# Output weights in a room of their own: loaded, gated and split during the attention, with the first output products ahead of the second row of merge work

## The chip, the cores and the metric

One core of one Trainium2 chip. The metric is the device time of one launch in microseconds (us). Five engines work side by side, each through its own list of instructions in order: TensorE (PE, matrix products), VectorE (DVE), ScalarE (ACT), GpSimd (POOL) and SyncE (SP). SP computes nothing here: its list holds most of the transfers between the chip's main memory and the core's buffer, and a transfer that has to wait for a buffer holds up every transfer behind it in that list.

## The reference

One layer of a diffusion block over 2048 tokens of width 1024, with 256 context tokens. Cut to what matters:

```python
fx, qx, kx, vx = split_projection(hx @ w_in)
y_four = fourier_mix(fx)                                        # 2048 x 512
y_attn = neighbourhood_attention(qx, kx, vx, kc, vc, rpb)       # 2048 x 512, 8 heads
g_f, g_a = split(sigmoid(hx @ w_gate))
merged = g_f * (y_four @ w_fourier_out) + g_a * (y_attn @ w_attn_out)
x = x + g1 * (merged @ w_out)                                   # w_out: 1024 x 1024
hx2 = modulate(rms_norm(x, norm2_g), sh2, sc2)
x = x + g2 * (relu(hx2 @ w_mlp1) ** 2 @ w_mlp2)
```

A factor of a product is kept as two f16 tiles, a high part H and a low rest L, and a product is made of three matmuls (H by H, H by L, L by H).

## The kernel before

The program runs in stages: projections, Fourier mixer, attention, merge, MLP. Loops in Python write the whole program out, a scheduler with a timeline of its own then sets the order on each engine; at run time each engine goes through its list in order and waits on semaphores. What is said below of orders is what the built program holds.

**Attention.** 64 steps (head pair 0 to 3, block of rows 0 to 3, block of columns 0 to 3), each with two heads. A head's block runs: scores `sc` on PE, bias and minimum on DVE (line 1312, tile `s`), exponential on ACT (1316), transposes `tp` on PE, high part `pH` on ACT, low part `pL` on DVE (1333), values `pv` on PE, scaling `yp` on ACT (1342). The queries of a block of rows are eight transfers, `Q` and `Ql` of two heads, put into SP's list one step of four ahead by `fetch`, which chains its transfers in program order.

**Filler.** Between the blocks a generator, `beside_attention`, yields small pieces of other work: first the Fourier half of the merge (`pmf`), then `load_wa`, then `attn_out(0)`. `load_wa` brings the four blocks of `w_attn_out` through the staging tile `wst`, of which there are two buffers, and scales and splits them on POOL:

```python
def load_wa():
    for k in range(4):
        wt = pm.tile([128, D], F32, tag="wst", name=f"wao{k}", bufs=2)
        fetch(wt, a["w_attn_out"][0, k * 128:(k + 1) * 128, :])
        pool.tensor_scalar(wt, wt, mgs[:, 0:1], None, op0=ALU.mult)
        pool.tensor_copy(wa[0][:, k, :], wt)
        pool.tensor_tensor(wa[1][:, k, :], wt, wa[0][:, k, :], op=ALU.subtract)
```

**Merge.** The 2048 tokens are cut into eight rows of W = 256. `attn_out(t)` loads the attention's result of row t into a `wst` buffer (`yat`), splits it (`yaH`, `yaL`), makes eight products `pua` (12 matmuls of 128x256 each), and forms the gated sum as `mH`, `mL`, with `gf`, `ft` and `ga` loaded for each pair of products. `out_proj(t, i)` multiplies half a row with the output weights: two products `po` of 24 matmuls of 128x512, added to `x1` (a tile of x) on DVE, stored, and normed on ACT. `norm_T(t)` transposes the normed row and writes the MLP's input. In steady state the loop runs out_proj(t), attn_out(t+2), norm_T(t).

**The output weights.** `wo` holds `w_out` times the gate `g1r` as H and L, in the pool `pg`, which is opened only when the attention's pools are closed. Eight blocks `wou0` to `wou7` of 512 KB are staged in `wst` and in `xh`, multiplied on DVE (line 1534), copied to H on ACT (1535), and subtracted to L on POOL or DVE in turn (1536). This stands in program order between the pieces of `attn_out(1)`; `out_proj(0, 0)` comes after it.

**Start of the MLP.** Four of seven parts of its input (`hc`) have room early. The other three, and the two `raw` buffers for weights still to be prepared, lie in the pool `pr`, opened when `pg` is closed.

Of the kernel before, what the change touches and what calls it, by code (L numbers as in the profile page):

```python
# [19 lines left out]
D = 1024  # L20
# [43 lines left out]
def dit_block(ctx: ExitStack, tc: tile.TileContext, a, out, taps=None, upto=9):  # L64
# [3 lines left out]
    def sbuf(name, side="left"):  # L68
        return tc.alloc_tile_pool(name=name, bufs=1, side=side, reuse_waits="tile")
# [7 lines left out]
    def mm3(ps, ops, start=True, stop=True):  # L77
        n = 3 * len(ops)
        i = 0
        for lh, ll, rh, rl in ops:  # L80
            for l, r in ((lh, rh), (lh, rl), (ll, rh)):
                last_mm[0] = pe.matmul(ps, l, r, start=(start and i == 0), stop=(stop and i == n - 1))  # L82
                i += 1
# [964 lines left out]
    def fetch(dst, src):  # L1048

        with tc.issue_after(in_order[0].ins):  # L1050
            in_order[0] = sp.dma_start(dst, src)
# [301 lines left out]
            act.dma_start(yA[hp, :, rb * 512:(rb + 1) * 512], yo)  # L1353

    W = 256
    pm = wa = None
    merged = {}

    def attn_out(t, ps_pool, m_pool):
# [35 lines left out]
            pool.tensor_tensor(wa[1][:, k, :], wt, wa[0][:, k, :], op=ALU.subtract)  # L1395
# [62 lines left out]
    def out_proj(t, i):  # L1458
        mH, mL = merged[t]
        r0 = t * W + i * 128  # L1460
        nm = f"{t}_{i}"
        cs = slice(i * 128, (i + 1) * 128)
        x1 = x1s.pop(0)
        load_x1()
        for n in range(2):
            ns = slice(n * 512, (n + 1) * 512)
            ps = mmp.tile([128, 512], F32, tag="mm", name=f"po{nm}_{n}")
            mm3(ps, [(mH[:, k, cs], mL[:, k, cs], wo[0][:, k, ns], wo[1][:, k, ns]) for k in range(KT)])
# [50 lines left out]
        put(1, b21)  # L1519

    NT = S // W
    def stage_wo(k):

        p_, tag = ((pm, "wst"), (pg, "xh"))[k % 2]
        t = p_.tile([128, D], F32, tag=tag, name=f"wou{k}", bufs=2)
        sp.dma_start(t, a["w_out"][0, k * 128:(k + 1) * 128, :])
        return t


    attn = attn_out(1, mmp, pg)  # L1530
    for k in range(8):
        next(attn)
        wt = stage_wo(k)
        dve.tensor_tensor(out=wt, in0=wt, in1=g1r, op=ALU.mult)
        act.activation(wo[0][:, k, :], wt, AF.Copy)
        (pool, dve)[k % 2].tensor_tensor(out=wo[1][:, k, :], in0=wt, in1=wo[0][:, k, :], op=ALU.subtract)  # L1536
    for _ in attn:
        pass
    load_x1()
    load_x1()  # L1540
    for t in range(NT - 2):
        out_proj(t, 0)
        out_proj(t, 1)
        for _ in attn_out(t + 2, mmp, pg):
            pass
        norm_T(t)
    pm.release()

# [8 lines left out]

    def load_hc(half, part, then=None):
        r = {}
        for c in (PRODUCTS[:4], PRODUCTS[4:])[part]:  # L1560
# [135 lines left out]
    def small(name):  # L1696
        return pr.tile([128, 512], F32, tag="wo", name=name, bufs=5)

    prep = prepare(jobs, lambda n_: pr.tile([128, 2048], F32, tag="raw", name=n_, bufs=2), lambda n_: pr.tile([128, 512], F32, tag="wt", name=n_),
                   lambda n_: small(n_).bitcast(F16).rearrange("p (c n) -> p c n", c=1), 1, act.dma_start, pool.dma_start)  # L1700
    acc, banks = {}, {}

# [84 lines left out]
    for i, s in enumerate(slots):  # L1787
# [20 lines left out]
    for p_ in (pr, p2p, pl, mmp):  # L1808
        p_.release()


# [52 lines left out]
```

## Time and profile before

| what | us |
|---|---|
| runs | 2658.70, 2662.83, 2666.41 (median 2662.83) |
| the profiled execution, its own time | 2660.88 |
| its span, first to last instruction | 2659.1 |
| PE busy in the span | 2538.6 (95%) |
| DVE, ACT, POOL busy | 1827.3, 1183.3, 484.4 |
| last low part `pL` of the attention begins | 1213.28 |
| first matmul of `attn_out(2)`, start of the steady merge | 1261.34 |
| first matmul of the MLP | 1482.09 |

The profiled execution lies 1.95 us under the median, and 1.8 us of its time lie outside its span. All places in time below are from the span's start. PE's row counts matmuls as they overlap, so that 95% does not say that PE runs at its best; idle time of PE is what the waits and the windows are read for.

### The profile page before, as it was taken

The numbers are of one execution on the slowest core, as the hardware profiler recorded it, in microseconds if no ns is written. First come the engines' busy times: TensorE is split into PE (matmuls) and PEld (weight loads), VectorE is DVE, ScalarE is ACT, GpSimd is POOL, SyncE is SP. The second block draws the span as 40 slices with busy tenths as digits, with TensorE's granted clock in tenths as the row PEclk, the third lists the DMA queues.
The fourth block names the chain that finished last, engine by engine and source line by source line (L and its number), as shares of the span: only waits on it lengthen the run. The fifth ranks groups of instructions, "written<-read, shape, count | busy, mean of one in ns | idle before, by whom it ended". The sixth has DMA issues, their size and how long they took to land.

```text
span 2659.1 us, 42665 instructions
## 1 busy us (share of the span) xinstructions
PE 2538.6 (95%) x15830; PEld 1473.0 (55%) x15830; DVE 1827.3 (69%) x3672; ACT 1183.3 (44%) x2113; POOL 484.4 (18%) x715
## 2 busy tenths in 40 slices
PE   6899989898999899998999999999999999999999
PEld 5445756776656678875666444444444444444444
DVE  6756976568553678887777696978877644636367
ACT  5623225545242577874444564627351333314050
POOL 1201221012224545452000121121211100000000
PEclk9999999999999999998999999999999999999999
DMA  8577689867374744556767777787766533333334
GB/s 269 137 225 204 203 248 304 270 204 245 93 249 141 199 118 138 148 169 207 237 226 264 260 242 261 231 279 233 268 235 230 181 99 105 101 103 99 104 103 155
DMA packets 345962, 517.77 MB, mean 195 GB/s; under 512 B 48497, under 2 KB 210505, under 8 KB 341401
## 3 DMA queue, kind: packets, MB, share of 16 engines
q1 hardware_dynamic: 296425, 406.50, 48.8%
q0 software_dynamic: 29104, 75.23, 8.4%
q10 hardware_dynamic: 20224, 33.31, 3.9%
q8 instruction: 124, 2.03, 0.3%
q14 instruction: 85, 0.70, 0.1%
HBM read 370.11 MB, written 145.84 MB: 194 GB/s over the span
## 4 chain that ended last, share of the span: by engine, by line
PE 68%; DMA 11%; DVE 11%; issue 3%; ACT 3%; POOL 3%; SPq 2%; DVEq 0%; ACTq 0%; POOLq 0%
PE p L82 21%; PE pm L82 17%; PE ps_g L82 8%; PE po L82 6%; DMA w12m<-in_w_mlp 3%; PE pua L82 2%; PE ps_k L82 2%; PE tp L1325 2%; PE pmf L1263 2%; PE pv L1339 1%; SPq L188 1%; PE ps_f L82 1%; PE ps_v L82 1%; PE sc L1303 1%; DVE wo L387 1%
## 5 line engine op out<-in xcount | busy, mean ns | idle before, releaser
L82 PE MATMUL pm<-hc,wb 128*128 128x512 f16 x2688 | 582.6, 379 | 5.6 <-DVE p L1605 2.1
L82 PE MATMUL p<-wb,a 128*128 128x512 f16 x2688 | 581.9, 379 | 2.1 <-DVE X L1605 1.5
L82 PEld LDWEIGHTS <-wb 128*128 128x128 f16 x2688 | 262.9, 98 | 323.6 <-issue 7.3
L82 PEld LDWEIGHTS <-a 128*128 128x128 f16 x2688 | 263.0, 98 | 319.7 <-issue 2.9
L82 PE MATMUL ps_g<-hx,w_g 128*128 128x512 f16 x1536 | 342.5, 380 | 0.9 <-ACT ot_f L516 0.9
L1605 DVE TENSOR_TENSOR X<-X,p 128x512 f32<-128x512 f32 x280 | 184.5, 685 | 171.1 <-PE p L82 151.8
L82 PEld LDWEIGHTS <-hx 128*128 128x128 f16 x2304 | 227.4, 99 | 39.6 <-issue 7.2
L82 PEld LDWEIGHTS <-w_g 128*128 128x128 f16 x1536 | 151.0, 99 | 171.2 <-issue 3.2
L1091 POOL DMA_DIRECT2D bt<-tT x264 | 132.4, 508 | 76.3 <-DVE ri L1332 53.0
L1605 DVE TENSOR_TENSOR u<-pm,u 128x512 f32<-128x512 f32 x128 | 87.5, 690 | 84.3 <-PE pm L82 82.5
L1312 DVE CUSTOM_DVE_ANT_0 s<-sc,bt,qsc 128x736 f32<-128x736 f32 (+5 forms) x128 | 111.2, 869 | 37.1 <-PE sc L1306 33.9
L386 ACT ACTIVATE wo<-ws,msc 128x512 f16<-128x512 f32 x96 | 69.0, 718 | 152.0 <-DVE ws L430 124.0
L1609 ACT ACTIVATE p<-pm 128x512 f32<-128x512 f32 x32 | 18.9, 589 | 239.7 <-PE pm L82 239.7
L1739 POOL DMA_DIRECT2D xr<-x1d x32 | 17.3, 539 | 569.8 <-DVE X L1605 562.1
L1333 DVE SCALAR_TENSOR_TENSOR pL<-tp,pH 128x640 f16<-128x640 f32 (+1 forms) x128 | 112.3, 878 | 5.0 <-ACT pH L1328 4.5
L1316 ACT ACTIVATE s<-s,m 128x736 f32<-128x736 f32 (+5 forms) x128 | 104.6, 817 | 16.5 <-DVE m L1312 13.9
L386 ACT ACTIVATE wo<-raw,msc 128x512 f16<-128x512 f32 x128 | 87.4, 709 | 52.0 <-DVE raw L430 17.8
L82 PE MATMUL po<-wouH,mH 128*128 128x512 f16 x256 | 97.3, 384 | 9.3 <-DVE ga L1383 9.3
L1325 PE MATMUL tp<-ident,s 128*128 128x128 f32 x704 | 103.1, 281 | 0.8 <-ACT s L1316 0.7
L516 ACT ACTIVATE ot_g<-ps_g,usc_g 128x512 f32<-128x512 f32 x64 | 43.4, 681 | 130.9 <-PE ps_g L82 117.6
L82 PE MATMUL po<-wouL,mH 128*128 128x512 f16 x256 | 98.8, 386 | 2.4 <-POOL wouL L1536 2.4
L387 DVE SCALAR_TENSOR_TENSOR wo<-raw,msc,wo 128x512 f16<-128x512 f32 x128 | 94.4, 748 | 8.0 <-ACT wo L386 7.9
(535 smaller groups left out, 4645.9 us busy)
## 6 DMA issues: line engine op xcount, KB each, us to landing
wb<-w1d SPq DMA_DIRECT2D x224, 256.0 KB
wb<-w2d SPq DMA_DIRECT2D x224, 256.0 KB
w12m<-in_w_mlp SPq DMA_DIRECT2D x32, 1024.0 KB
raw<-in_w_mlp ACTq DMA_DIRECT2D x24, 1024.0 KB
w1d<-wo POOLq DMA_DIRECT2D x84, 256.0 KB, 4.0
w2d<-wo POOLq DMA_DIRECT2D x84, 256.0 KB, 4.0
gT<-ot_g SPq DMA_DIRECT2D x64, 256.0 KB
hc<-hcd SPq DMA_DIRECT2D x14, 1024.0 KB
```

The costliest lines, as they stand in the source:

```text
L82: last_mm[0] = pe.matmul(ps, l, r, start=(start and i == 0), stop=(stop and i == n - 1))
L188: last_load[0] = sp.dma_start(dst, src)
L386: act.activation(hi, src, AF.Copy, scale=scale)
L387: dve.scalar_tensor_tensor(out=lo, in0=src, scalar=scale, in1=hi, op0=ALU.mult, op1=ALU.subtract)
L516: act.activation(o, ps, func, scale=scale)
L1091: load_(t[i * 16:(i + 1) * 16, :, off + j0 * w:off + (j0 + 8) * w], raw(tT[ct], (2 * hp * 15 + dr) * w, [[120 * w, 16], [15 * w, 2], [1, 8 ...
L1263: pe.matmul(ps, l, r, start=(i == 0), stop=(i == len(prods) - 1))
L1312: tail["dve"] = dve.tensor_tensor_reduce(out=s[:, :n], in0=sc, in1=bias, op0=ALU.add, op1=ALU.min, scale=qsc[:, 4:5], scalar=3.0e38, accum ...
L1316: tail["act"] = act.activation(s[:, :n], s[:, :n], AF.Exp, bias=m1[:, 0:1], scale=-1.0, accum_out=m1[:, 1:2])
L1325: tail["pe"] = pe.transpose(tp[:, i * 128:(i + 1) * 128], s[:, o:o + 128], ident)
L1333: tail["dve"] = dve.scalar_tensor_tensor(out=pL[:, :c], in0=tp[:, :c], scalar=PTOP, in1=pH[:, :c], op0=ALU.mult, op1=ALU.subtract)
L1605: last["dve"] = dve.tensor_tensor(out=o, in0=x, in1=y, op=op)
```

## The change

The output weights get a left-side pool `mgw` (`pw`), opened with the merge's pool while the attention still runs. `beside_attention` loads, gates and splits the eight blocks right after `load_wa` and ahead of `attn_out(0)`, all through the two `wst` buffers and with `fetch`. After the attention out_proj(0, 0) comes ahead of `attn_out(1)`, and out_proj(0, 1) ahead of `attn_out(2)`. At the start of the MLP three `hc` parts and one of the two `raw` buffers move into `pw`, in the place of `wo`.

```diff
     def beside_attention():
-        nonlocal pm, wa
+        nonlocal pm, pw, wa, wo
         yield from merge_fourier()
         mf.release()
+        pw = sbuf("mgw")
         pm = sbuf("mga")
         wa = [pm.tile([128, 4, D], F16, tag="wa" + o, name="wa" + o) for o in "HL"]
         load_wa()
+        wt = pw.tile([128, 8, D], F16, tag="woH", name="wouH")
+        wo = [[wt[:, k] for k in range(8)], []]
+        for i in range(2):
+            wt = pw.tile([128, 4, D], F16, tag=f"woL{i}", name=f"wouL{i}")
+            wo[1] += [wt[:, k] for k in range(4)]
+        for k in range(8):
+            wt = pm.tile([128, D], F32, tag="wst", name=f"wou{k}", bufs=2)
+            fetch(wt, a["w_out"][0, k * 128:(k + 1) * 128, :])
+            yield
+            dve.tensor_tensor(out=wt, in0=wt, in1=g1r, op=ALU.mult)
+            act.activation(wo[0][k], wt, AF.Copy)
+            (pool, dve)[k % 2].tensor_tensor(out=wo[1][k], in0=wt, in1=wo[0][k], op=ALU.subtract)
         while n < order.index((3, 0, 3)) + 3:
             yield
         yield from attn_out(0, mmp, pm)
...
-    wo = [pg.tile([128, 8, D], F16, tag="wo" + o, name="wou" + o) for o in "HL"]
...
-    attn = attn_out(1, mmp, pg)
-    for k in range(8):
-        next(attn)
-        wt = stage_wo(k)
-        dve.tensor_tensor(out=wt, in0=wt, in1=g1r, op=ALU.mult)
-        act.activation(wo[0][:, k, :], wt, AF.Copy)
-        (pool, dve)[k % 2].tensor_tensor(out=wo[1][:, k, :], in0=wt, in1=wo[0][:, k, :], op=ALU.subtract)
-    for _ in attn:
-        pass
+    def attn_rows(t):
+        for _ in attn_out(t, mmp, pg):
+            pass
     load_x1()
     load_x1()
-    for t in range(NT - 2):
+    for i in range(2):
+        out_proj(0, i)
+        attn_rows(1 + i)
+    norm_T(0)
+    for t in range(1, NT - 2):
...
-            r[c] = (pr if part else pl).tile([128, 4, 2, 4, 128], F16, tag=f"hc{c}", name=f"hc{half}_{c}")
+            if part == 0:
+                r[c] = pl.tile([128, 4, 2, 4, 128], F16, tag=f"hc{c}", name=f"hc{half}_{c}")
+            else:
+                if i != 1:
+                    room = pw.tile([128, 2 - i // 2, 4, 2, 4, 128], F16, tag=("woH", "woL0")[i // 2], name=f"hc{half}_{c}")
+                r[c] = room[:, i % 2]
...
+        return (pr, pw)[len(raws) % 2].tile([128, 2048], F32, tag=("raw", "woL1")[len(raws) % 2], name=name)
```

What it moves in the built program, at three places. In the names below a number behind the last underscore is the tile's own; `Q3_2_0` are the queries of head pair 3, block of rows 2, first head; `sc6_2_0` and `s0` are the scores of head 6, rows 2, columns 0.

SP's list before, from the last two blocks of `w_attn_out` to the first load of `attn_out(0)`:

```order
L1051 DMA wao2_14408<-in_w_attn_out 128x1024
L1051 DMA wao3_14413<-in_w_attn_out 128x1024
L1051 DMA Q3_2_0_14577<-qH_59 64x512 x2
L1051 DMA Ql3_2_0_14580<-qL_60 64x512 x2
L1051 DMA Q3_2_1_14583<-qH_59 64x512 x2
L1051 DMA Ql3_2_1_14586<-qL_60 64x512 x2
L1051 DMA yat0_14725<-yA_75 128x4x256
```

SP's list now, at the same place (each `wou` but the first two needs the `wst` buffer of the `wou` two ahead of it):

```order
L1051 DMA wao3_14416<-in_w_attn_out 128x1024
L1051 DMA wou0_14424<-in_w_out 128x1024
L1051 DMA wou1_14473<-in_w_out 128x1024
L1051 DMA wou2_14515<-in_w_out 128x1024
L1051 DMA wou3_14561<-in_w_out 128x1024
L1051 DMA wou4_14566<-in_w_out 128x1024
L1051 DMA wou5_14608<-in_w_out 128x1024
L1051 DMA Q3_2_0_14610<-qH_59 64x512 x2
L1051 DMA Ql3_2_0_14613<-qL_60 64x512 x2
L1051 DMA Q3_2_1_14616<-qH_59 64x512 x2
L1051 DMA Ql3_2_1_14619<-qL_60 64x512 x2
L1051 DMA wou6_14675<-in_w_out 128x1024
```

Six loads of output weights now stand ahead of the queries of the next block of rows, and two more (`wou6`, `wou7`) between them and `yat0`.

DVE's list before, from the last low part of the block of columns 2 (rows 1) to the first score of the next block of rows and the low part behind it:

```order
L1333 SCALAR_TENSOR_TENSOR pL7_1_2_14869<-tp7_1_2_14861,pH7_1_2_14868 128x768
L1312 ISA s0_9428,m16_2_0_14932<-sc6_2_0_14927,bt1_9323,qsc_136 128x616
L1312 ISA m16_2_0_14932 128x1
L1332 RECIPROCAL ri6_1_3_14934<-m16_1_3_14825 128x1
L1333 SCALAR_TENSOR_TENSOR pL6_1_3_14925<-tp6_1_3_14917,pH6_1_3_14924 128x768
```

DVE's list now, from the same instruction to the same first score:

```order
L1333 SCALAR_TENSOR_TENSOR pL7_1_2_14915<-tp7_1_2_14907,pH7_1_2_14914 128x768
L1415 TENSOR_TENSOR wou0_14424<-wou0_14424,g1r_132 128x1024
L1415 TENSOR_TENSOR wou1_14473<-wou1_14473,g1r_132 128x1024
L1417 TENSOR_TENSOR wouL0_14422<-wou1_14473,wouH_14421 128x1024
L1415 TENSOR_TENSOR wou2_14515<-wou2_14515,g1r_132 128x1024
L1415 TENSOR_TENSOR wou3_14561<-wou3_14561,g1r_132 128x1024
L1417 TENSOR_TENSOR wouL0_14422<-wou3_14561,wouH_14421 128x1024
L1415 TENSOR_TENSOR wou4_14566<-wou4_14566,g1r_132 128x1024
L1415 TENSOR_TENSOR wou5_14608<-wou5_14608,g1r_132 128x1024
L1312 ISA s0_9428,m16_2_0_14978<-sc6_2_0_14973,bt1_9323,qsc_136 128x616
```

All eight steps on `wou0` to `wou5` stand between two neighbouring blocks of the attention. On ACT the six copies to `wouH` stand in one run at the same place, and `wou6` and `wou7` follow on both engines between the next scores: both products ahead of `s2` of head 6, columns 1.

DVE's list before, from the attention's last `pL` on, first rows:

```order
L1333 SCALAR_TENSOR_TENSOR pL7_3_3_15732<-tp7_3_3_15725,pH7_3_3_15731 128x640
L1386 TENSOR_TENSOR mL0_14732<-ga0_6_15252,mH0_14731 128x256
L1376 TENSOR_TENSOR ft1_2_15858<-ft1_2_15858,gf1_2_15857 128x512
L1383 SCALAR_TENSOR_TENSOR ga1_0_15805<-pua1_0_15812,mgs_142,ga1_0_15805 128x256
L1534 TENSOR_TENSOR wou2_15880<-wou2_15880,g1r_132 128x1024
L1384 SCALAR_TENSOR_TENSOR ga1_0_15805<-ft1_0_15807,mgs_142,ga1_0_15805 128x256
```

DVE's list now, from the same instruction on:

```order
L1333 SCALAR_TENSOR_TENSOR pL7_3_3_15778<-tp7_3_3_15771,pH7_3_3_15777 128x640
L1386 TENSOR_TENSOR mL0_14778<-ga0_6_15298,mH0_14777 128x256
L1376 TENSOR_TENSOR ft1_2_15959<-ft1_2_15959,gf1_2_15958 128x512
L1482 SCALAR_TENSOR_TENSOR x1_0_15841<-po0_0_0_15847,mgs_142,x1_0_15841 128x512
L1482 SCALAR_TENSOR_TENSOR x1_0_15841<-po0_0_1_15873,mgs_142,x1_0_15841 128x512
L1383 SCALAR_TENSOR_TENSOR ga1_0_15916<-pua1_0_15923,mgs_142,ga1_0_15916 128x256
```

The weights' steps are gone from here, and the two products of out_proj(0, 0) come out ahead of the first of `attn_out(1)`; PE's list has them in the same order, `po0_0` (48 matmuls), `pua1` (96), `po0_1` (48), `pua2`.

More of the change, by code (lines that the diff above doesn't have):

```diff
@@ L1355, in dit_block @@
     W = 256
-    pm = wa = None
+    pm = pw = wa = wo = None
     merged = {}
@@ L1467, in out_proj @@
             ps = mmp.tile([128, 512], F32, tag="mm", name=f"po{nm}_{n}")
-            mm3(ps, [(mH[:, k, cs], mL[:, k, cs], wo[0][:, k, ns], wo[1][:, k, ns]) for k in range(KT)])
+            mm3(ps, [(mH[:, k, cs], mL[:, k, cs], wo[0][k][:, ns], wo[1][k][:, ns]) for k in range(KT)])
             dve.scalar_tensor_tensor(out=x1[:, ns], in0=ps, scalar=mgs[:, 3:4], in1=x1[:, ns], op0=ALU.mult, op1=ALU.add)
@@ L1521, in dit_block @@
     NT = S // W
[L1522 to L1527, printed above, removed]
-    attn = attn_out(1, mmp, pg)
-    for k in range(8):
-        next(attn)
-        wt = stage_wo(k)
-        dve.tensor_tensor(out=wt, in0=wt, in1=g1r, op=ALU.mult)
-        act.activation(wo[0][:, k, :], wt, AF.Copy)
-        (pool, dve)[k % 2].tensor_tensor(out=wo[1][:, k, :], in0=wt, in1=wo[0][:, k, :], op=ALU.subtract)
-    for _ in attn:
-        pass
+    def attn_rows(t):
+        for _ in attn_out(t, mmp, pg):
+            pass
     load_x1()
     load_x1()
-    for t in range(NT - 2):
+    for i in range(2):
[3 more added lines that the diff above has]
+    for t in range(1, NT - 2):
         out_proj(t, 0)
         out_proj(t, 1)
-        for _ in attn_out(t + 2, mmp, pg):
-            pass
+        attn_rows(t + 2)
         norm_T(t)
@@ L1559, in load_hc @@
         r = {}
-        for c in (PRODUCTS[:4], PRODUCTS[4:])[part]:
-            r[c] = (pr if part else pl).tile([128, 4, 2, 4, 128], F16, tag=f"hc{c}", name=f"hc{half}_{c}")
+        for i, c in enumerate((PRODUCTS[:4], PRODUCTS[4:])[part]):
+            if part == 0:
[4 more added lines that the diff above has]
+                r[c] = room[:, i % 2]
             i = sp.dma_start(r[c].rearrange("p s o k t -> p s (o k t)"), hcd[half][c])
@@ L1807, in dit_block @@
                 steps += 1
-    for p_ in (pr, p2p, pl, mmp):
+    for p_ in (pr, p2p, pl, pw, mmp):
         p_.release()
```

5 lines of the change are left out of this document (4 added, 1 removed).

## The prediction

> **What bounds the kernel now.** First the windows by stage: the attention's last 14 us before the place in question, the rest of it, the gap up to the steady merge, one steady period, and the start of the MLP.
>
> ```profile
> core 0: us, PE busy (x) PEld busy (x) DVE busy (x) ACT busy (x) POOL busy (x), PEclk, DMA share, GB/s
> 1150.00:1164.00 14.00, 13.61 (x197) 11.69 (x194) 13.53 (x32) 13.66 (x32) 12.41 (x7) 1.00 0.34 112
> 1164.00:1214.00 50.00, 43.81 (x578) 37.83 (x578) 42.41 (x95) 36.22 (x82) 17.35 (x11) 0.97 0.47 148
> 1214.00:1261.30 47.30, 35.94 (x198) 20.00 (x199) 32.56 (x47) 14.53 (x21) 16.94 (x5) 0.86 0.72 248
> 1316.00:1349.00 33.00, 33.00 (x210) 20.63 (x209) 25.34 (x51) 14.62 (x26) 1.48 (x2) 1.00 0.69 234
> 1485.00:1575.00 90.00, 83.07 (x388) 37.90 (x386) 75.04 (x120) 58.47 (x100) 15.01 (x28) 1.00 0.77 259
> ```
>
> In the steady merge PE never idles. The one stretch near the change where it does is 1214 to 1261: 11.4 of 47.3 us idle, at a granted clock of 0.86. At 1150 to 1164 all three engines of the attention are 97% busy: nothing that is put there is free. Next PE's waits from 1150 to 1262:
>
> ```profile
> PE po L82 <- DVE ga L1383: 8.8, 1, 8.8
> PE po L82 <- POOL wouL L1536: 2.4, 1, 2.4
> PE pua L82 <- POOL yaL L1366: 1.9, 1, 1.9
> PE sc L1303 <- DMA Q<-qH: 1.9, 1, 1.9
> PE pua L82 <- ACT yaH L1365: 0.8, 1, 0.8
> ```
>
> The first two are the weights' work in the way of the merge: DVE does both, and PE waits for `ga` behind it. That is what the change takes away. The fourth is the one to watch: a score waiting for its queries. SP's and DVE's timelines say why.
>
> ```profile
> 1158.33 2.44 SPq L1051 DMA_DIRECT2D wao<-in_w_attn_out  x2
> 1160.87 1.09 SPq L1051 DMA_DIRECT2D Q<-qH  x2
> 1164.61 1.19 SPq L1051 DMA_DIRECT2D Ql<-qL  x2
> 1172.14 0.38 SPq L1051 DMA_DIRECT2D yat<-yA  x1
> ```
>
> ```profile
> 1163.38 0.94 DVE L1333 SCALAR_TENSOR_TENSOR pL<-tp,pH 128x768 f16<-128x768 f32 x1
> 1166.48 0.86 DVE L1312 CUSTOM_DVE_ANT_0 s<-sc,bt,qsc 128x616 f32<-128x616 f32 x1 [2.16 <-PE sc L1306]
> 1170.18 0.98 DVE L1312 CUSTOM_DVE_ANT_0 s<-sc,bt,qsc 128x736 f32<-128x736 f32 x1
> ```
>
> The queries stand behind the last two `wao` loads, which wait for a `wst` buffer; they go out at 1160.87, and `s0` runs 5.6 us later, 2.16 us late already. Attention has no queries to spare here.
>
> **The change, part by part.**
>
> *The queries now stand behind six more loads.* `wou0` takes the buffer that `yat` takes before (free at 1172.14); `wou1` that of the last `wao`, whose subtraction ends at 1174.2. Each later load needs the buffer two loads back: landed, gated, copied, subtracted.
>
> ```profile
> 1162.01 2.84 POOL L1393 TENSOR_SCALAR wao<-wao,mgs 128x1024 f32<-128x1024 f32 x1 [1.59 <-DMA wao<-in_w_attn_out]
> 1169.98 4.23 POOL L1395 TENSOR_TENSOR waL<-wao,waH 128x1024 f16<-128x1024 f32 x2
> ```
>
> ```profile
> 1160.44 4.60 DMA wao<-in_w_attn_out
> 1213.40 4.93 DMA wou<-in_w_out
> 1239.09 9.95 POOL wouL L1536
> 1347.78 13.17 PE po L82 x61
> 1360.94 10.48 PE pua L82 x96
> ```
>
> ```profile
> L1534 DVE TENSOR_TENSOR wou<-wou,g1r x8: 1212/1217/1224, 1192.4 to 1242.4; 128x1024 f32<-128x1024 f32 x8
> L1535 ACT ACTIVATE wouH<-wou x8: 1041/1057/1058, 1220.7 to 1243.6; 128x1024 f16<-128x1024 f32 x8
> L1536 POOL TENSOR_TENSOR wouL<-wou,wouH x4: 2115/2217/9937, 1221.8 to 1249.0; 128x1024 f16<-128x1024 f32 x4
> L1536 DVE TENSOR_TENSOR wouL<-wou,wouH x4: 1214/1216/1218, 1230.3 to 1245.8; 128x1024 f16<-128x1024 f32 x4
> ```
>
> A load of 512 KB took 3.6 us (issued at 1158.33, POOL starts on it at 1162.01), 4.60 and 4.93 in the chain; two overlap here as the first two of these did, so I take 4.1. An even round is 4.1 + 1.22 (DVE) + 1.06 (ACT) + 2.12 (POOL) + 0.2 for four hand-overs = 8.7 us. POOL's subtraction falls on DVE's product of the odd load, 2 us behind. The 9.95 us subtraction in the chain shows POOL held up while DVE ran two-input work, so I add 1.0: 9.7 us a round. The end without collision is 8.2 (load 3.6), the other 10.7 (load 4.9, collision and hand-overs 1.4).
>
> The Trainium skill, "SBUF — State Buffer", section "Who interferes with whom", says that a DVE instruction with two SBUF inputs and a GpSimd one that reads SBUF exclude each other for the whole instruction. By that rule a collision costs up to the 1.22 us of the DVE product, and three rounds without it would be 3 us shorter; the 9.95 us row agrees with it, none shows this pair alone.
>
> So `wou2` goes at 1181.8, `wou4` at 1191.5. The odd round (DVE subtracts, 1.22) is shorter: `wou5` goes right behind, the queries at 1192.3 instead of 1160.87: **+31.4 us** (28.4 to 33.4 by the two rounds' ends). All of it is on the path: in DVE's list the six products, in ACT's the six copies stand ahead of `s0`, PE's next scores need the queries, and no other product is ready, since `yat0` comes later still.
>
> The Trainium skill, "DMA: Bandwidth & Descriptors", section "Anatomy of one DMA", fits 2.0 us plus bytes over 436 GB/s to transfers issued by GpSimd; an estimate for 512 KB is 3.2 us, and the sum would be some 3 us less. These loads are issued by SP and the rows show 3.6 to 4.9, so the rows decide.
>
> *`wou6`, `wou7` and `yat0`.* Round three ends at 1201.2, `wou6` lands and is gated by 1206.5, `wou7` by 1207.7, and only then DVE may do `s2`, at 1170.18 before: +37.5, so **+6.1** (+4 to +8). `yat0` needs `wou6`'s buffer: copy and POOL's subtraction end at 1209.7; landing takes 3.7 (issued 1249.06, used 1252.77), and ACT does `yaH0` until 1214.5 ahead of a `yp` that ran at 1174.67: +39.8, **+2.3** (0 to +4).
>
> ```profile
> 1249.06 0.36 SPq L1362 DMA_DIRECT2D yat<-yA  x1
> ```
>
> ```profile
> 1174.67 0.30 ACT L1342 ACTIVATE yp<-pv,ri 128x64 f32<-128x64 f32 x1
> 1252.77 1.06 ACT L1365 ACTIVATE yaH<-yat 128x1024 f16<-128x1024 f32 x1 [8.10 <-DMA yat<-yA]
> ```
>
> *What the attention gets back.* The two waits for `yaH` and `yaL` (2.7 us) go, since both come earlier in the lists, and the half-rate matmuls after them (0.42 instead of 0.27 us, some 1.6 us). `wou0`'s product leaves the attention (1.22), and a `ga` of 1.49 us beside POOL's `ft` shrinks by 1.0: **-6.5** (-4 at worst).
>
> ```profile
> 1192.40 1.22 DVE L1534 TENSOR_TENSOR wou<-wou,g1r 128x1024 f32<-128x1024 f32 x1
> 1193.53 1.49 DVE L1384 SCALAR_TENSOR_TENSOR ga<-ft,mgs,ga 128x256 f32<-128x256 f32 x1
> ```
>
> Against that PE starts again after 30 us of rest. After 8.82 us of it the clock was at half for twelve matmuls, 5.1 us where 2.6 would do:
>
> ```profile
> 1233.89 0.61 PE L82 MATMUL po<-wouH,mH 128*128 128x512 f16 x1 [8.82 <-DVE ga L1383]
> 1238.99 0.38 PE L82 MATMUL po<-wouH,mH 128*128 128x512 f16 x1
> 1184.54 0.42 PE L82 MATMUL pua<-yaH,waH 128*128 128x256 f16 x1
> 1261.34 0.27 PE L82 MATMUL pua<-yaH,waH 128*128 128x256 f16 x1
> ```
>
> So **+2.5** (0 to +5). The attention ends 31.4 + 6.1 + 2.3 - 6.5 + 2.5 = 35.8 us later.
>
> *The stretch after it.* From 1214 to 1261.3 PE must do 96 `po` and 96 `pua`. At the steady rate: 96 x 13.17 / 61 = 20.7, and 10.5, in all 31.2; the attention's last `pv` and `ty` take some 1.1. So of 47.3 us **-15.0** can go. Its covers: out_proj(0, 0) needs only `mH0`, `mL0` and finished weights, and its 10.4 us hide the loads for `attn_out(1)`. What could come in the way: in SP's list the store of `x1_0` and the load of `x1_384` stand ahead of the last `ft1` and `ga1`; up to 4 us, so -11 to -16.
>
> *Start of the MLP.* PE idles 6.9 of 90 us there, and one wait is for `raw`:
>
> ```profile
> PE pm L82 <- DMA raw<-in_w_mlp: 1.5, 1, 1.5
> ```
>
> One `raw` load now goes out about when the last `po` ends. I take that wait: **-1.5** (-7, all the idle time, to +3, since ACT's and DVE's order there changes and DVE is 83% busy).
>
> *Edits that cost nothing*: the same eight loads and products are made once as before; `norm_T(0)` and the later rows keep their order, and the steady period its 33 us.
>
> Sum on the profiled execution's own time, 2660.9: +35.8 - 15.0 - 1.5 = +19.3, **2680 us**. The median of the runs shown lies 2 us above that execution. With all low ends: 28.4 + 4 + 0 - 6.5 + 0 - 16 - 7 = +3; with all high ends: 33.4 + 8 + 4 - 4 + 5 - 11 + 3 = +38.
>
> **The rivals.**
>
> *Faster: only the arithmetic counts.* If the queries were out in time, the attention would pay DVE's twelve operations, 12 x 1.22 = 14.6 us, less the 6.5 it gets back, and the stretch after it gains 15.0: 14.6 - 6.5 - 15.0 - 1.5 = -8.4, 2652. For it: DVE's work does leave the place where PE waits for it. Against it: SP's rows, where the queries go only after the second `wao` got its buffer. It decides at an attention ending 16.5 us later in all: the six loads would have to be through by about 1173, when the first has just gone out.
>
> *No change: the merge gives back what the queries cost.* It needs rounds of some 5 us, a load of less than 1 us beside 4.4 us of arithmetic; or idle time at the MLP of 6.9 us gone as well and both rounds at their low end, which is +3.
>
> *Slower still: the next queries are late too.* `Q3_3` stands behind `yat0` and six loads for `attn_out(0)`: by the sum its first four are out at about 1216 and landed by 1219, and they are needed at about 1223. Beyond 4 us of lag each further us is paid; with 10 more, 2690, with rounds of 10.7 up to 2700.
>
> *The change doesn't do what it says*: if the weights' steps hid in the stall the attention has at the queries already, 2.16 us, only the row swap would count. The gap is a tenth of three rounds.
>
> **How the numbers follow.** Forecast 0.76; slower still 0.12; no change 0.07; faster 0.05. A measurement of this kernel tells about 0.3%, 8 us, from no change. Of the forecast some 0.03 lies less than 8 us above 2663. Slower by more than that: the two slower cases without it, 0.85; within: 0.07 + 0.03 = 0.10; faster: 0.05. The range, 2665 to 2698, takes the forecast's bounds from +4 to +37 and the near part of the slower rival; some 0.12 is left out by the cases of no gain or loss and 0.06 beyond the top.
>
> **What would show it.** In the profile after: PE idle for 28 to 34 us at about 1164 to 1197, ended by a wait of `sc` for `Q`; six `wou` loads on SP some 2 and 8 us apart in turn, before `Q`; `yat` on SP about 37 us later than 1172; then from the last `pL` to the first `pua` of the third row about 32 us instead of 47. The prediction is wrong if the queries go out before 1180, if the stretch after the attention doesn't shrink by 10 us, or if the MLP's start moves by more than 7.

## The result, and the profile after

The change makes the kernel slower by about half a percent. Five runs of the changed kernel gave a median of 2674.89 us against 2661.10 us before (ratio 1.0055, 95% interval 1.0037 to 1.0073). A second set of six, taken later beside the experiments, gave 2681.62 us against 2662.35 (1.0066, 1.0049 to 1.0083). Over all eleven the median is 2680.75 us; within one set the single runs of a kernel lie 5 to 19 us apart.

To compare executions, places are counted from one instruction that comes ahead of the change's effect on the attention in all of them but one (told there): the low part `pL` of the step just before `s0` (the "reference point"). It lies at 1163.38 us before and at 1164.23 after. In the later execution of the changed kernel it lies at 1159.33, 4.9 us earlier. The two spans also differ by 4.9 us (2679.0 and 2674.1), but single parts behind the reference point differ by 2 to 3 us either way and only nearly cancel.

PE's waits in the changed kernel, from 1150 to 1280 us (total, number, longest; two of eight rows):

```profile
PE sc L1303 <- DMA Q<-qH: 31.8, 1, 31.8
PE po L82 <- DVE ga L1383: 0.5, 1, 0.5
```

One wait of a score for its queries, 1.9 us before, is now 31.8. The waits of the output products for `ga` (8.8 us) and for `wouL` (2.4) are gone or nearly so. SP's list around the queries, with start and length of the issue (an issue that waits for a buffer is long; rows between these are left out):

```profile
1159.18 2.43 SPq L1051 DMA_DIRECT2D wao<-in_w_attn_out  x2
1172.43 19.91 SPq L1051 DMA_DIRECT2D wou<-in_w_out  x6
1192.43 1.09 SPq L1051 DMA_DIRECT2D Q<-qH  x2
1207.49 0.38 SPq L1051 DMA_DIRECT2D yat<-yA  x1
```

Six loads hold SP for 19.91 us, and the queries go out right behind them; `yat`, at 1172.14 before, goes at 1207.49. DVE and POOL in the same stretch, with the idle time before an operation and what ended it in brackets (rows between are left out here too):

```profile
1175.95 1.23 DVE L1415 TENSOR_TENSOR wou<-wou,g1r 128x1024 f32<-128x1024 f32 x1 [10.79 <-DMA wou<-in_w_out]
1178.74 2.81 DVE L1415 TENSOR_TENSOR wou<-wou,g1r 128x1024 f32<-128x1024 f32 x1 [1.56 <-DMA wou<-in_w_out]
1184.05 1.22 DVE L1415 TENSOR_TENSOR wou<-wou,g1r 128x1024 f32<-128x1024 f32 x1 [0.15 <-DMA wou<-in_w_out]
1195.94 1.74 DVE L1415 TENSOR_TENSOR wou<-wou,g1r 128x1024 f32<-128x1024 f32 x1 [2.62 <-DMA wou<-in_w_out]
1197.74 0.86 DVE L1312 CUSTOM_DVE_ANT_0 s<-sc,bt,qsc 128x616 f32<-128x616 f32 x1
```

```profile
1178.35 2.12 POOL L1417 TENSOR_TENSOR wouL<-wou,wouH 128x1024 f16<-128x1024 f32 x1 [3.86 <-ACT wouH L1416]
1186.44 2.12 POOL L1417 TENSOR_TENSOR wouL<-wou,wouH 128x1024 f16<-128x1024 f32 x1 [5.97 <-ACT wouH L1416]
```

The even products start 8.1 us apart (1175.95, 1184.05): that is one round of a buffer. `s0` runs at 1197.74, 33.5 us behind the reference point where it was 3.1.

The windows from the reference point to the last `pL` of the attention, and from there to the third row of the merge, first before, then after (window, length, busy times, granted clock, DMA share, GB/s):

```profile
1163.38:1213.28 49.90, 44.06 (x582) 37.93 (x579) 42.31 (x97) 36.84 (x83) 17.97 (x11) 0.97 0.47 149
1213.28:1261.34 48.06, 36.07 (x201) 20.00 (x199) 33.28 (x48) 14.53 (x21) 16.98 (x5) 0.86 0.72 246
```

```profile
1164.23:1245.90 81.67, 44.94 (x570) 38.63 (x568) 58.02 (x108) 44.68 (x90) 26.09 (x15) 0.79 0.46 143
1245.90:1279.12 33.22, 32.71 (x213) 19.93 (x214) 16.95 (x36) 7.73 (x16) 0.59 (x1) 1.00 0.69 235
```

The attention takes 31.8 us more with nearly the same PE work (44.9 us busy for 44.1). The stretch behind it takes 14.8 us less, and PE is busy in all but 0.5 us of it. Both halves of the change's story are in these four rows.

### The profile page after: what moved, and what is told of

Same layout as the page of the kernel before. It is cut to its first block, busy times and chain, and to the rows that moved or that the text cites. A ratio compares the mean times of both kernels' runs of the same rounds, so it can differ in the third digit from the quotient of the medians.

```text
span 2679.0 us, 42663 instructions
## 1 busy us (share of the span) xinstructions
PE 2536.9 (95%) x15830; PEld 1472.7 (55%) x15830; DVE 1825.8 (68%) x3672; ACT 1182.9 (44%) x2113; POOL 477.3 (18%) x715
## 4 chain that ended last, share of the span: by engine, by line
PE 65%; DMA 12%; DVE 10%; issue 4%; POOL 3%; ACT 2%; SPq 1%; DVEq 0%; ACTq 0%; POOLq 0%
PE p L82 21%; PE pm L82 18%; PE ps_g L82 8%; PE po L82 6%; DMA w12m<-in_w_mlp 4%; PE pua L82 2%; PE ps_k L82 2%; PE tp L1325 2%; PE pmf L1263 2%; PE pv L1339 1%; PE sc L1303 1%; DVE wo L387 1%; DMA Q<-qH 1%; DMA raw<-in_w_mlp 1%; DVE aaccg L276 1%
## 5 line engine op out<-in xcount | busy, mean ns | idle before, releaser
L1312 DVE CUSTOM_DVE_ANT_0 s<-sc,bt,qsc 128x736 f32<-128x736 f32 (+5 forms) x128 | 111.1, 868 | 35.3 <-PE sc L1306 31.8
L82 PE MATMUL po<-wouH,mL 128*128 128x512 f16 x256 | 97.0, 379 | 0.0
```

The source lines that it names most:

```text
L1312: tail["dve"] = dve.tensor_tensor_reduce(out=s[:, :n], in0=sc, in1=bias, op0=ALU.add, op1=ALU.min, scale=qsc[:, 4:5], scalar=3.0e38, accum ...
```

## The experiments

Each kernel is told by its two windows, cut at the same instructions as above; with them the median of its runs and the ratio to the kernel before on the same chip.

| kernel | attention, us | stretch, us | sum | median, us | ratio (95%) |
|---|---|---|---|---|---|
| before | 49.9 | 48.1 | 98.0 | 2660.4 to 2662.5 | |
| changed | 81.7 | 33.2 | 114.9 | 2674.9 | 1.0055 (1.0037 to 1.0073) |
| changed, again | 83.8 | 32.6 | 116.4 | 2681.6 | 1.0066 (1.0049 to 1.0083) |
| old order of rows | 83.5 | 35.1 | 118.6 | 2680.8 | 1.0083 (1.0063 to 1.0103) |
| order of rows alone | 49.3 | 52.1 | 101.4 | 2662.0 | 1.0013 (0.9999 to 1.0028) |
| rooms alone | 54.3 | 42.7 | 97.0 | 2659.5 | 1.0002 (0.9986 to 1.0018) |
| four own buffers | 71.4 | 34.2 | 105.5 | 2667.5 | 1.0025 (1.0011 to 1.0039) |
| two pieces each | 69.5 | 40.8 | 110.3 | 2676.6 | 1.0051 (1.0034 to 1.0069) |
| late, own buffers | 63.9 | 32.9 | 96.8 | 2662.0 | 0.9993 (0.9979 to 1.0007) |
| no loads | 76.3 | 32.9 | 109.2 | 2677.2 | 1.0057 (1.0033 to 1.0081) |
| no loads, own buffers | not counted (see there) | 33.2 | | 2677.0 | 1.0048 (1.0033 to 1.0062) |
| own buffers, all on POOL | 82.9 | 32.9 | 115.7 | 2682.1 | 1.0076 (1.0055 to 1.0098) |
| late, subtraction on POOL | 56.9 | 39.1 | 96.0 | 2656.8 | 0.9982 (0.9967 to 0.9996) |
| late, all on POOL | 55.0 | 42.7 | 97.7 | 2663.0 | 1.0004 (0.9991 to 1.0016) |

The theory: the queries stand in SP's list behind loads that wait for two shared buffers, and the attention stands still for it. The rivals: the arithmetic put into a busy attention; the order of rows; the new rooms at the MLP's start.

**The changed kernel again.** No edit.

> The changed kernel itself once more, beside the others of this set: its five times fell into two groups, 2674.6 to 2674.9 and 2680.8 to 2683.4, and the comparisons with variants need its middle. If the profiled execution was of the ordinary kind: 2680 in the median. If the lower group is: 2675. The attention from the reference point lasts 80 to 83 us in either case.

The median is 2681.6. The six times lie between 2675.9 and 2689.1 and fill the gap between the two groups that I had seen, so they are not two kinds of run. The query wait is 31.8 us in this execution too; the attention lasts 83.8 us, just over the 80 to 83 that I had said.

**The old order of rows.**

```diff
-    for i in range(2):
-        out_proj(0, i)
-        attn_rows(1 + i)
-    norm_T(0)
-    for t in range(1, NT - 2):
+    attn_rows(1)
+    for t in range(NT - 2):
```

> The changed kernel with the old order of rows: out_proj(0, 0) comes behind attn_out(1) again; the weights stay in the attention. If the queries behind the loads are the loss, the attention is as in the changed kernel (queries out at about 1192, last pL at about 1246), and only the stretch up to the first product of the third row changes: 33.2 us in the changed kernel, 48.1 before. I expect 38 (PE has to wait for yat1, which the swap covered with 10 us of output products, but no longer for the weights), so some 2680. If the swap earns all of the 15 us: 48 and 2690. If the weights' leaving earns all: 33 and 2675.

```profile
1163.42:1246.94 83.52, 44.88 (x570) 38.68 (x568) 60.28 (x107) 44.89 (x90) 25.94 (x15) 0.78 0.44 140
1246.94:1282.02 35.08, 32.67 (x212) 19.68 (x213) 17.65 (x37) 7.85 (x16) 0.59 (x1) 1.00 0.69 233
```

The stretch is 35.1 us: of the 15 us that it lost, 13 come from the weights' leaving it, and about 2 from the new order. I had expected 5 of it from the order. The time cannot be told from that of the changed kernel.

**The order of rows alone.** The kernel before, with the loop of the changed one and the weights built after the attention as before.

```diff
-    attn = attn_out(1, mmp, pg)
     for k in range(8):
-        next(attn)
...
-    for _ in attn:
-        pass
+    def attn_rows(t):
+        for _ in attn_out(t, mmp, pg):
+            pass
+
     load_x1()
     load_x1()
-    for t in range(NT - 2):
+    for i in range(2):
+        out_proj(0, i)
+        attn_rows(1 + i)
+    norm_T(0)
+    for t in range(1, NT - 2):
```

> The kernel before with the new order of rows alone; the weights are built after the attention. The attention keeps its times (queries at about 1161, last pL at 1213). out_proj(0, 0) then needs all eight weights at once, which were covered by the products of attn_out(1): from the last pL to the third row 55 to 60 us instead of 48, in all some 2668 to 2673. If the swap by itself were the gain of the stretch: 35 us and 2648. If order does not count: 48 and 2661.

PE's waits from the last `pL` to the third row, where a product of the weights is now needed at once:

```profile
PE po L82 <- ACT wouH L1533: 8.0, 3, 4.4
PE po L82 <- DVE wouL L1534: 2.8, 2, 2.5
PE po L82 <- POOL wouL L1534: 1.4, 2, 1.2
```

The stretch is 52.1 us, 4.1 more than before and less than the 55 to 60 that I had expected; so is the time, 2662.0, whose interval just reaches no change. The order is no gain by itself: the products of the second row covered the weights' preparation.

**The rooms alone.** The weights lie in `pw` and the MLP's parts follow them there, while loads and arithmetic stay after the attention.

```diff
-            fetch(wt, a["w_out"][0, k * 128:(k + 1) * 128, :])
-            yield
...
+    for k in range(8):
+        next(attn)
+        wt = stage_wo(k)
```

> The kernel before with the new rooms alone: the output weights lie in the pool opened during the attention, the three hc parts and one raw buffer move into it at the start of the MLP; loads, arithmetic and order of rows are as before. Up to the first product of the MLP nothing changes (1482). By the prediction the MLP ends 1.5 us earlier (2659.5); by the profile of the changed kernel, in which that part came out longer, 2.4 us later (2663.5). A difference under 3 us between the medians tells neither; then the MLP's span in the trace decides.

The times are the same. From the first product of the MLP to the end it takes 1177.4 us, and 1177.0 before. In the two executions of the changed kernel that part takes 1179.4 and 1176.2, with the old order of rows 1175.3. So the rooms are worth nothing that these runs show; my -1.5 and the first execution's +2.4 both lie within what one program varies by. The wait of PE for `raw` (1.5 us before) is indeed not among PE's waits in the first 90 us of the MLP in any of these executions; the MLP is no shorter for it. The built program has some of the weights' loads earlier than before, three of them inside the attention where one was; with that, 4 to 5 us moved from the stretch into the attention.

**Four staging buffers of their own.**

```diff
-            wt = pm.tile([128, D], F32, tag="wst", name=f"wou{k}", bufs=2)
+            wt = pm.tile([128, D], F32, tag="wos", name=f"wou{k}", bufs=4)
```

> The changed kernel with four staging buffers of the output weights' own instead of the two wst. Four loads can go out before the step in question; the queries stand only behind wou4 and wou5, which need the buffers of wou0 and wou1, free at about 1169. If the wait for the loads is the loss, queries go out at 1169 to 1172 instead of 1192, and the time falls by 17 to 23 us, to about 2655. If the added arithmetic on DVE and ACT is the loss, it stays, as the same twelve operations and copies stand ahead of s0: 2671 to 2675. If the attention regains time whatever the queries do, 2665.

```profile
1159.57 2.42 SPq L1051 DMA_DIRECT2D wao<-in_w_attn_out  x2
1162.04 18.35 SPq L1051 DMA_DIRECT2D wou<-in_w_out  x6
1180.48 1.09 SPq L1051 DMA_DIRECT2D Q<-qH  x2
```

```profile
1171.86 3.14 DVE L1417 TENSOR_TENSOR wouL<-wou,wouH 128x1024 f16<-128x1024 f32 x1
```

```profile
1170.83 3.09 POOL L1417 TENSOR_TENSOR wouL<-wou,wouH 128x1024 f16<-128x1024 f32 x1
```

The queries go out 15.9 us behind the reference point instead of 28.2, and the attention is 10.3 us shorter. That is the theory's direction, but half its size (I had said 1169 to 1172, it was 1180.5). Two things were missing in my sum. The first loads go out only at 1162, since they too stand behind the two `wao` loads in SP's list. And with loads in hand POOL and DVE work at the same time: an operation of 1.22 us on DVE takes 3.14, one of 2.12 on POOL 3.09. The time, 2667.5, lies 12 us above the 2655 that I had given this case.

**Two filler pieces for each block.**

```diff
             fetch(wt, a["w_out"][0, k * 128:(k + 1) * 128, :])
             yield
+            yield
```

> The changed kernel with two filler pieces instead of one for each block of the output weights. In SP's list the queries then stand behind three loads instead of six, the other five behind the queries and ahead of the next block of rows' queries. Nothing else of the weights' work changes: the same two buffers, the same twelve DVE operations. If the loads ahead of the queries are the loss: the third load goes out at about 1180, the queries at 1181 instead of 1192, and some 11 us come back, of which part is lost again where DVE waits for later loads: 2662 to 2668. If the arithmetic is the loss: 2675. If all that counts is the buffers' chain, wherever it stands, 2675 too, but with the stall in two pieces.

```profile
1174.73 8.32 SPq L1051 DMA_DIRECT2D wou<-in_w_out  x3
1183.14 1.09 SPq L1051 DMA_DIRECT2D Q<-qH  x2
1188.16 20.62 SPq L1051 DMA_DIRECT2D wou<-in_w_out  x5
```

With three loads ahead instead of six the queries go out 16.6 us behind the reference point, and the attention is 12.1 us shorter: the place in SP's list is the cause of the stall. But the stretch gets 7.6 us longer, as the later pieces push products of the first row out of the attention (PE is busy in the stretch for 38.1 us instead of 32.7), and the time, 2676.6, hardly moves; I had said 2662 to 2668.

**Late, in buffers of their own.** The queries now stand behind two loads that wait for nothing; the other six stand behind them.

```diff
+        for _ in range(4):
+            yield
         for k in range(8):
-            wt = pm.tile([128, D], F32, tag="wst", name=f"wou{k}", bufs=2)
+            wt = pm.tile([128, D], F32, tag="wos", name=f"wou{k}", bufs=4)
             fetch(wt, a["w_out"][0, k * 128:(k + 1) * 128, :])
             yield
+            if k % 2:
+                yield
```

> The changed kernel with the weights' pieces begun four filler pieces later and spread (an extra piece behind every second block), in four staging buffers of their own. The queries stand behind two loads that wait for nothing, and go out at 1162 to 1164, as in the kernel before; no load waits long for a buffer. What is left is the arithmetic: twelve DVE operations of 1.22 us or up to 3.1 where POOL runs beside them, less 6.5 us the attention gets back. If waiting for loads is the loss, the attention lasts 55 to 64 us from the reference point (49.9 before, 81.7 in the changed kernel), the stretch after it 33: 2650 to 2661. If the arithmetic is: 75 us and 2670.

```profile
1158.70 1.17 SPq L1051 DMA_DIRECT2D Q<-qH  x2
1165.45 17.51 SPq L1051 DMA_DIRECT2D wou<-in_w_out  x6
1183.05 1.09 SPq L1051 DMA_DIRECT2D Q<-qH  x2
```

```profile
PE sc L1303 <- DVE m L1312: 12.1, 6, 3.9
PE sc L1303 <- DMA Q<-qH: 4.6, 1, 4.6
```

```profile
1160.22:1224.10 63.88, 47.17 (x567) 40.09 (x566) 60.24 (x104) 43.48 (x89) 30.76 (x15) 0.89 0.55 177
1224.10:1256.98 32.88, 32.55 (x222) 20.00 (x219) 19.39 (x40) 8.90 (x17) 0.59 (x1) 1.00 0.75 247
```

The queries go out 1.5 us ahead of the reference point, 2.5 before. I had expected that no load waits long, and that is not so: six loads hold SP's list for 17.51 us, but now ahead of the next queries, and no score waits for those. The query wait falls from 31.8 to 4.6 us, and the loss against the kernel before is gone: 0.9993, an interval around no change. But the attention comes back to 63.9 us, not to 49.9. Scores now wait for DVE, which is busy for 60.24 of 63.88 us. Under the stall lay the arithmetic, which the stall had hidden; taking 27.2 us off the wait gave back 18 to 20 us of the attention.

**No loads.** The rival of the arithmetic, by itself: no load stands anywhere, the operations do. The weights' values are left out.

```diff
-            fetch(wt, a["w_out"][0, k * 128:(k + 1) * 128, :])
             yield
-            dve.tensor_tensor(out=wt, in0=wt, in1=g1r, op=ALU.mult)
+            dve.tensor_tensor(out=wt, in0=g1r, in1=g1r, op=ALU.subtract)
```

> The changed kernel without the eight loads of the output weights; the staging tile is filled by a DVE operation of the same kind and size from a tile that is there, so all arithmetic, buffers and copies stay, and the weights' values are left out. The scheduler then sets the twelve DVE operations as one group behind the fourth score step of the block of rows. The theory says that the queries go out at 1161 and the attention pays the group alone, 15 to 25 us with POOL's subtractions of 2.1 to 3.1 us between, less 6.5: 58 to 68 us from the reference point, 2653 to 2664. If the attention takes the group for nothing (PE has products in store), 50 us and 2645. If the arithmetic is all of the loss, 80 us and 2675.

```profile
1158.53 1.09 SPq L1051 DMA_DIRECT2D Q<-qH  x2
1201.23 0.38 SPq L1051 DMA_DIRECT2D yat<-yA  x1
```

```profile
PE pua L82 <- ACT yaH L1365: 25.2, 1, 25.2
```

```profile
1198.00 3.21 POOL L1416 TENSOR_TENSOR wouL<-wou,wouH 128x1024 f16<-128x1024 f32 x1 [2.43 <-ACT wouH L1415]
```

This is a miss, and the most useful one. The queries are on time, no load is in the way, and the time is as bad as the changed kernel's. PE now waits 25.2 us in another place: `yat0` needs a `wst` buffer, and the weights' chain holds both until POOL's last subtraction ends at 1201.21; `yat` goes out at 1201.23. The rounds run on arithmetic alone, 5.6 us each. So a loss of this size needs no loads: a long chain through two buffers that others need is enough. The arithmetic alone is not priced by this run, as it stands in that chain.

**No loads, own buffers.** The same, the weights' values left out again, with four staging buffers of the weights' own.

```diff
-            wt = pm.tile([128, D], F32, tag="wst", name=f"wou{k}", bufs=2)
+            wt = pm.tile([128, D], F32, tag="wos", name=f"wou{k}", bufs=4)
```

> The kernel without the weights' loads (the staging tile is filled by a DVE operation from a tile that is there; the weights' values are left out) with four staging buffers of its own, so that yat0 no longer waits for a buffer that the weights hold. With the two shared buffers PE waited 25 us for yaH and the attention lasted 76.3 us from the reference point. If that wait is the shared buffers', it goes: what is left is the arithmetic, 14.6 us and some us of POOL's interference, less 6.5: 58 to 66 us, 2655 to 2664. If the arithmetic on DVE, ACT and POOL itself is the 25 us, it stays: 74 us or more, 2672 to 2678.

```profile
1192.68 2.40 SPq L1051 DMA_DIRECT2D wao<-in_w_attn_out  x2
1195.18 1.09 SPq L1051 DMA_DIRECT2D Q<-qH  x2
```

```profile
PE sc L1303 <- DMA Q<-qH: 25.8, 1, 25.8
PE pua L82 <- ACT yaH L1365: 0.6, 1, 0.6
```

The wait for `yaH` goes, as said, but the time does not fall: 2677.0. With nothing to wait for, the scheduler set the weights' group ahead of the reference point, and their subtractions ahead of the work on `wao` in POOL's list. That work now frees the shared buffers late, the last two `wao` loads go out at 1192.7 instead of 1158.3, and the queries stand behind them. It is the same stall through a third door, so this run does not price the arithmetic either: the time falls into the range that I had given for the arithmetic being all of it, by another way. The attention is not counted from the reference point here, since the weights' group stands ahead of it.

**Own buffers, all on POOL.** Loads issued by POOL, three buffers of their own, and gating and subtraction on POOL.

```diff
-            wt = pm.tile([128, D], F32, tag="wst", name=f"wou{k}", bufs=2)
-            fetch(wt, a["w_out"][0, k * 128:(k + 1) * 128, :])
+            wt = pm.tile([128, D], F32, tag="wos", name=f"wou{k}", bufs=3)
+            pool.dma_start(wt, a["w_out"][0, k * 128:(k + 1) * 128, :])
             yield
-            dve.tensor_tensor(out=wt, in0=wt, in1=g1r, op=ALU.mult)
+            pool.tensor_tensor(out=wt, in0=wt, in1=g1r, op=ALU.mult)
             act.activation(wo[0][k], wt, AF.Copy)
-            (pool, dve)[k % 2].tensor_tensor(out=wo[1][k], in0=wt, in1=wo[0][k], op=ALU.subtract)
+            pool.tensor_tensor(out=wo[1][k], in0=wt, in1=wo[0][k], op=ALU.subtract)
```

> The changed kernel with the loads issued by POOL, three staging buffers of their own, and gating and subtraction both on POOL; ACT still copies, DVE does nothing for the weights. The queries and yat stand behind no load of the weights. POOL has 16 operations of 2.1 to 3.1 us, 34 to 50 us, beside its other 18 us of the 50 us attention. If waiting for loads and DVE's share are the loss, the attention lasts 50 to 58 us and the time is 2645 to 2655. If POOL's port holds DVE's two-input operations up for as long as it works, the attention lasts 65 to 75 us: 2660 to 2670. If POOL's work does not end in time, the first output product waits for it: up to 10 us more.

```profile
1156.91 7.00 POOL L1415 TENSOR_TENSOR wou<-wou,g1r 128x1024 f32<-128x1024 f32 x3
```

```profile
1174.22 2.41 SPq L1051 DMA_DIRECT2D wao<-in_w_attn_out  x2
1176.72 1.09 SPq L1051 DMA_DIRECT2D Q<-qH  x2
```

None of my three cases: no weights' load stands in SP's list, and still the queries go out 17 us later than in the kernel before (14.5 us behind the reference point, 2.5 ahead of it there). POOL's list now has the gating ahead of the work on `wao`, the last two `wao` loads wait for their buffers until 1174.2, and the queries stand behind them, as above. That is 17 of the 33 us that this attention is longer. For the rest, `s0` runs 10.8 us behind the queries' issue, 5.6 before, with loads that POOL issues under way, and from `s0` to the end it takes 57.6 us, 46.8 before; what costs these 16 us was not taken apart.

**Late, subtraction on POOL.** The late variant with

```diff
-            (pool, dve)[k % 2].tensor_tensor(out=wo[1][k], in0=wt, in1=wo[0][k], op=ALU.subtract)
+            pool.tensor_tensor(out=wo[1][k], in0=wt, in1=wo[0][k], op=ALU.subtract)
```

> The late, spread variant with four buffers of its own (attention 63.9 us from the reference point, 49.9 before), with all eight subtractions on POOL: DVE has eight operations for the weights instead of twelve, ACT the same eight copies. If what is left of the loss is DVE's time, the attention gets 4 x 1.22 = 4.9 us shorter, 59 us, and the time 2655 to 2658 against the late variant's 2662. If ACT's copies (8.5 us) or POOL's interference bound it, 62 to 66 us and 2660 to 2664.

```profile
1162.38:1219.29 56.91, 43.10 (x532) 36.52 (x531) 49.57 (x92) 42.55 (x85) 36.92 (x18) 0.88 0.57 181
1219.29:1258.36 39.07, 36.39 (x250) 23.45 (x250) 23.02 (x47) 10.34 (x21) 1.98 (x2) 1.00 0.73 235
```

This is the fastest in the table: 2656.8 us, ratio 0.9982 (0.9967 to 0.9996), the time that I had said. The interval stops just short of no change and overlaps that of the late variant, so a gain over the kernel before is likely, and one over the late variant is not shown. DVE's time in the attention falls by 10.7 us, the attention by 7.0; but 6.2 go back into the stretch, where products of the first row that no longer fit in the attention are made (PE is busy there for 36.4 us instead of 32.6). The two windows together are 2.0 us under the kernel before.

**Late, all on POOL.** The same, with the gating on POOL too.

```diff
-            dve.tensor_tensor(out=wt, in0=wt, in1=g1r, op=ALU.mult)
+            pool.tensor_tensor(out=wt, in0=wt, in1=g1r, op=ALU.mult)
```

> The same late variant with gating and subtraction both on POOL, so that DVE does nothing for the weights; ACT copies. If DVE's time were all of what is left, the attention would last 50 to 53 us and the time 2648 to 2652. But POOL's sixteen operations, 35 us, stand between the casts that free the two shared buffers, and yat0 waits for one: if a shared buffer's owner being late is what costs, yat0 goes out 15 us later than in the kernel before, PE waits for yaH, and the attention lasts 62 to 70 us: 2660 to 2668.

```profile
PE sc L1303 <- DMA Q<-qH: 13.1, 2, 8.7
```

```profile
1170.43 23.86 SPq L1051 DMA_DIRECT2D wou<-in_w_out  x6
1194.38 1.09 SPq L1051 DMA_DIRECT2D Q<-qH  x2
```

DVE has no work for the weights, and the attention is 55.0 us. The wait for `yaH` that I had forecast is not there. The larger wait, 8.7 of 13.1 us, is for the next queries: six loads, held for 23.9 us by POOL's slower work on their buffers, stand ahead of `Q3_3`. The time lies in the range that I had given for the wait that did not come, which is luck. The time is that of the kernel before.

## Why the prediction was right, point by point

**The mechanism and the time.** Predicted 2680 us; measured 2674.9 and 2681.6 in two sets, 2680.75 over all. The wait is where it was put, of the size given (28 to 34 us said, 31.8 seen), and queries went out at 1192.43 (1192.3 said). The mechanism held; that the numbers fit so closely is in part luck, as the next points show. In the first execution the attention took 4.0 us less than said and the MLP 3.9 us more, and the two cancel.

**The queries, +31.4.** Counted from the reference point `s0` is later by 30.4 and 30.5 us in the two executions. The sum was right for partly wrong reasons. I took 9.7 us for an even round and it was 8.1, since the collision fell on DVE's product and not on POOL's subtraction (2.12 us, not lengthened). But that product belongs to the odd round, which I had put right behind the even one: the odd products start at 1178.74 and, two rounds on, at 1195.94, so 8.6 us a round, and this round, not the even one, sets when the sixth load goes out. It also starts 2.8 us behind the even one: 2.8 and 2 x 8.6 make 20.0 us where I had 2 x 9.7 and 0.8, 20.2. That the errors cancel is luck.

**`wou6`, `wou7`, +6.1**, read at `s2`: +4.0 in one execution and +6.4 in the other.

**`yat0`, what the attention gets back and the clock, together -1.7**: measured -2.6 and -3.0. So the attention ends 31.8 and 33.9 us later where I said 35.8.

**The stretch, -15.0**: -14.8 and -15.4. This is the term that was read from the profile most directly, as PE's work at the steady rate, and PE filled it.

**The MLP's start, -1.5**: +2.4 and -0.8; with the rooms alone +0.4. There is no gain there that these runs show; the wait for `raw` went, and the time did not follow. This term had the wrong size and, in the first execution, the wrong sign.

**The rivals.** "Only the arithmetic counts" gave 2652 for queries out in time. The late variant is that case, and it took 2662. The term that failed there is 12 x 1.22 = 14.6 us. DVE's eleven rows for the weights' twelve operations in that variant sum to 22.8 us; these are the first, the longest single one and the last:

```profile
1162.79 1.23 DVE L1419 TENSOR_TENSOR wou<-wou,g1r 128x1024 f32<-128x1024 f32 x1 [1.63 <-DMA wou<-in_w_out]
...
1182.05 3.14 DVE L1419 TENSOR_TENSOR wou<-wou,g1r 128x1024 f32<-128x1024 f32 x1
...
1195.41 1.21 DVE L1421 TENSOR_TENSOR wouL<-wou,wouH 128x1024 f16<-128x1024 f32 x1
```

The 8.2 us more are time spent beside POOL. With them the attention pays 22.8 - 6.5 = 16.3 by my formula, and 14.0 by the windows. "No change" needed rounds of some 5 us, and they were 8.1 and 8.6. "The next queries are late too" did not happen in the changed kernel, but it is what the last variant ran into.

**What the prediction did not see** is that the stall has more than one exit. I named the list that held the queries and took its removal for the cure. Three kernels with no load of the weights in SP's list at all still lose 15 to 20 us: one because the weights' chain holds the two `wst` buffers, two because POOL's list has the weights ahead of `wao`, which then holds them. What stays open is how much of the first row's products, pushed out of the attention wherever the pieces are spread, could be kept there; and a variant with both sets of queries ahead of all loads was not tried.

## What to carry to other kernels

Before work is moved into a busy stage, list for each buffer it borrows and each in-order list it enters who stands behind, and price the whole chain of rounds, not its operations: here 4.4 us of arithmetic for a block became a 20 us hold on the list that carried the queries. When a stall has been found, do not book its length as the gain of removing it; the work that ran under it comes to light (27.2 us less of wait gave back 18 to 20). Here the moved preparation did best with its own buffers, started after the urgent transfers were out, and with a third of its work taken off the engine that bounds the stage; done so, the change came out 0.2% faster instead of half a percent slower, which is close to what these runs can tell from nothing.

## What the hardware showed that was not expected

In most meetings, two-input operations of DVE and POOL took turns whole, in whichever order they came. In the changed kernel POOL's subtraction began at 1178.35 and DVE's product 0.39 us later: POOL kept its 2.12 us, DVE's 1.22 became 2.81. Without the loads both began at 1198.00: there DVE kept its 1.22 and POOL's 2.12 became 3.21, as this row of DVE and the one of POOL above show.

```profile
1198.00 1.22 DVE L1414 TENSOR_TENSOR wou<-g1r 128x1024 f32<-128x1024 f32 x1
```

The Trainium skill, "SBUF — State Buffer", section "Who interferes with whom", states that the pair of ports DVE shares with GpSimd is an exclusive lock; the rows agree, with a price of up to 1.9 us on DVE and up to 1.1 us on POOL in the meetings shown. In an attention bound by DVE that lock cost more (8.2 us in the late variant) than four of the twelve operations. One-input operations on POOL did it too: in the late variant a product of DVE that began at 1164.85 took 1.70 us behind a cast that POOL had begun at 1164.43.

One meeting went otherwise. In the kernel before, the subtraction that POOL began at 1239.09 took 9.95 us, while DVE ran without a gap from 1238.63 to 1247.06. POOL got no turn between DVE's operations there, as it did with four staging buffers at 1170.83; what makes the difference these runs do not show.
